# Softmax rows: from sixteen-row tiles in six buffers to thirty-two-row tiles in three, with one broadcast multiply a block

## The chip, the cores and the metric

The kernel runs on one core of one Trainium2 chip. The time is the device time in microseconds (us); most executions of one kernel agree within 0.3% (of the 38 of the kernel before, 162.08 to 163.24 us, 35 lie that close to their median, 162.5 us), and a change is called faster or slower when it is clear of 2%. The profile is one execution; its span is about 2 us shorter than the timed run (160.4 against 162.4 us here). Engines: DVE is VectorE, ACT is ScalarE; the DMA engines (16 of them) move data between HBM and SBUF; SP is the engine from whose queue the loads are issued.

Two executions were in a slower state, one of a_s2half (165.12 us, the fastest of that kernel 162.58) and one of copy64k (166.07 us, the fastest 163.52); they are left out of what follows.

## The reference

```python
x: (16, 1024, 512) float32
x_scaled = x / 0.5
exp_x = np.exp(x_scaled - np.max(x_scaled, axis=-1, keepdims=True))
return exp_x / np.sum(exp_x, axis=-1, keepdims=True)
```

That is 16384 rows of 512, read once and written once: 33.55 MB each way.

## The kernel before

A tile holds 16 rows on each of 128 partitions: 32 KiB a partition, contiguous in HBM, 4 MB in all. There are eight such chunks and six buffers, so the loads of six chunks are issued at the start, and the loads of the last two wait for the stores of the first two. (In the trace the first six go out in seven loads from 0.73 to 4.16 us; for the other two the load queue waited 75.1 us on stores, and the last went out at 88.3 us.) Work goes by blocks of 8 rows: DVE takes the row maxima of a block in one reduce, ACT makes the exponentials and the row sums row by row, DVE inverts the sums and scales three quarters of the rows, ACT scales the last quarter.

```python
G = 16                                              # rows of a partition in a tile
data = ctx.enter_context(tc.tile_pool(name="data", bufs=6))
BLOCKS = [(0, 8), (8, 8)]
...
def scale_vector(i):
    ...
    nc.vector.reciprocal(recip[:, 0:B], sums[:, 0:B])
    for g in range(B - B // 4):                      # one instruction a row
        nc.vector.tensor_scalar_mul(xb[:, g, :], xb[:, g, :], recip[:, g : g + 1])
...
def store(i):                                        # the whole chunk, issued on ACT
    c, b, B = blocks[i]
    if b + B == G:
        nc.scalar.dma_start(out=outr[c], in_=tiles[c])

for i in range(n + 3):
    if i < n:
        if blocks[i][1] == 0:
            load(blocks[i][0])                       # issued on SP
        shift(i)                                     # DVE: reduce, bias
        exponentials(i)                              # ACT
    if 1 <= i <= n:     scale_vector(i - 1)          # DVE
    if 2 <= i <= n + 1: scale_scalar(i - 2)          # ACT copies
    if 3 <= i:          store(i - 3)                 # one block after its copies
```

## Time and profile before

| | before |
|---|---|
| time, median of the first 3 runs | 162.37 us (162.35 to 162.6) |
| span of the profiled run | 160.4 us |
| bytes moved, rate from 4 to 156 us | 67.1 MB, 432 GB/s |
| DVE busy, ACT busy | 114.0 us, 113.1 us |
| first store issued, last store issued | 43.59 us, 137.05 us |

From the page of the kernel before: its span, the busy time of the engines with their share of the span, then rows of 40 equal slices of the span, in which a digit is the busy share in tenths (9 is 90% or more).

```profile
span 160.4 us, 517 instructions
...
DVE 114.0 (71%) x148; ACT 113.1 (70%) x290; POOL 0.2 (0%) x4
...
DVE  0608999999999999999999949996199946000000
ACT  3072579989999999999999995799709999100000
...
DMA  5999999999999999999999999999999999999993
```

The DMA row is full from the second slice to the last but one. DVE and ACT have finished by slice 35, and have holes before. The windows view of the same kernel says it for four stretches late in the run (columns: the stretch and its length, busy time and number of instructions of DVE, ACT and POOL, TensorE clock, DMA share, GB/s):

```profile
core 0: us, DVE busy (x) ACT busy (x) POOL busy (x), PEclk, DMA share, GB/s
60.00:116.00 56.00, 47.96 (x64) 51.40 (x132) 0.00 (x0) 1.00 1.01 437
116.00:120.00 4.00, 4.00 (x1) 0.00 (x0) 0.00 (x0) 1.00 0.95 410
120.00:126.00 6.00, 5.93 (x10) 5.54 (x15) 0.00 (x0) 1.00 1.01 437
126.00:132.00 6.00, 4.09 (x9) 5.83 (x17) 0.00 (x0) 1.00 1.01 437
```

So the kernel is bound by its transfers: 67.1 MB at 432 GB/s is 155 us, and the start and the end cost about 5 us more. The group of the multiplies by shape (count, then busy us and mean ns of one, then idle time before them), and the waits (us in total, times, longest):

```profile
L91 DVE TENSOR_SCALAR xt<-xt,recip 128x512 f32<-128x512 f32 x96 | 39.6, 482 | 0.6
```

```profile
ACT xt L75 <- DVE bias L67: 23.2, 16, 5.7
DVE negmax L65 <- DMA xt<-in_x_dram: 16.9, 4, 5.0
```

The multiplies show 482 ns each, but they overlap: the chain has six of them in 2.47 us, 0.41 us a row. The reduce of 4096 elements a partition takes 4.34 us in the chain, one element in 1.06 ns. Both from the chain (start, length, what):

```profile
27.17 2.47 DVE xt L91 x6
29.63 4.34 DVE negmax L65
```

ACT waits for DVE's bias 16 times; DVE waits for the loads, and only once, for 3.2 us, for ACT: of the two, DVE sets the pace.

### The profile page before, as it was taken

What the parts mean: (1) busy time and instruction counts of PE and PEld (TensorE: products, weight loads), DVE (VectorE), ACT (ScalarE), POOL (GpSimd) and SP (SyncE); (2) the same over time, 40 slices, a digit from 0 to 9 for tenths busy, and PEclk for the clock granted to TensorE, in tenths of its full rate; (3) what the DMA queues carried; (4) which work ended last, traced back from release to release, by engine and by line L of the source; (5) the groups of instructions that cost most, each with busy time, mean ns of one, the idle gap of its engine ahead of it and who ended that gap; (6) DMA issues with size and microseconds to landing.
All of it is one profiled execution on the core that took longest, in us unless ns stands there. A gap on an engine that the chain in (4) does not pass through costs nothing.

```text
span 160.4 us, 517 instructions
## 1 busy us (share of the span) xinstructions
DVE 114.0 (71%) x148; ACT 113.1 (70%) x290; POOL 0.2 (0%) x4
## 2 busy tenths in 40 slices
DVE  0608999999999999999999949996199946000000
ACT  3072579989999999999999995799709999100000
POOL 0000000000000000000000000000000000000000
DMA  5999999999999999999999999999999999999993
GB/s 190 464 425 490 392 417 490 403 392 507 409 368 417 386 441 474 392 417 474 417 409 476 417 400 490 417 400 458 441 409 441 458 409 433 458 400 425 474 409 155
DMA packets 2451, 67.13 MB, mean 419 GB/s; under 512 B 272, under 2 KB 272, under 8 KB 272
## 3 DMA queue, kind: packets, MB, share of 16 engines
q1 hardware_dynamic: 1296, 33.56, 49.4%
q10 hardware_dynamic: 1152, 33.55, 48.5%
q14 instruction: 3, 0.02, 0.0%
HBM read 33.55 MB, written 33.55 MB: 418 GB/s over the span
## 4 chain that ended last, share of the span: by engine, by line
DMA 43%; DVE 34%; ACT 7%; issue 1%; SPq 0%
DMA xt<-in_x_dram 24%; DVE negmax L65 23%; DMA out_dram<-xt 19%; DVE xt L91 9%; ACT xt L75 5%; ACT xt L98 2%; DVE bias L67 1%; DVE recip L89 0%; SPq L59 0%
## 5 line engine op out<-in xcount | busy, mean ns | idle before, releaser
L75 ACT ACTIVATE xt<-xt,bias 128x512 f32<-128x512 f32 x128 | 90.5, 708 | 23.2 <-DVE bias L67 23.2
L65 DVE TENSOR_REDUCE negmax<-xt 128x8 f32<-128x4096 f32 (+1 forms) x17 | 70.8, 4163 | 16.9 <-DMA xt<-in_x_dram 16.9
L91 DVE TENSOR_SCALAR xt<-xt,recip 128x512 f32<-128x512 f32 x96 | 39.6, 482 | 0.6
L75 ACT ACTIVATION_READ_ACCUMULATOR xt<-xt,bias 128x1 f32 x128 | 23.9, 187 | 0.0
L98 ACT ACTIVATE xt<-xt,recip 128x512 f32<-128x512 f32 x32 | 21.0, 707 | 0.0
L89 DVE RECIPROCAL recip<-sums 128x8 f32<-128x8 f32 (+1 forms) x17 | 3.3, 192 | 3.2 <-ACT xt L75 3.2
L67 DVE TENSOR_SCALAR bias<-negmax 128x8 f32<-128x8 f32 (+1 forms) x17 | 2.9, 171 | 0.6
L50 ACT ACT_TABLE_LOAD x1 | 1.3, 1283 | 0.7 <-PEq L134 0.7
L49 DVE MEMSET warm<- 128x1 f32 x1 | 0.1, 59 | 0.8 <-PEq L134 0.8
L50 ACT ACTIVATE warm<-warm 128x1 f32<-128x1 f32 x1 | 0.2, 203 | 0.0
L134 POOL MEMSET const-bfloat16-1.0<- 128x1 bf16 x1 | 0.1, 102 | 0.0
L134 POOL MEMSET const-uint8-127<- 128x1 uint8 x1 | 0.1, 101 | 0.0
L134 POOL MEMSET const-float32-0.0<- 128x1 f32 x1 | 0.1, 99 | 0.2 <-issue 0.2
L134 POOL MEMSET const-float32-1.0<- 128x1 f32 x1 | 0.1, 98 | 0.0
## 6 DMA issues: line engine op xcount, KB each, us to landing
out_dram<-xt ACTq DMA_DIRECT2D x8, 4096.0 KB, 26.2
xt<-in_x_dram SPq DMA_DIRECT2D x7, 4096.0 KB, 30.3
xt<-in_x_dram SPq DMA_DIRECT2D x1, 3072.0 KB, 11.5
xt<-in_x_dram SPq DMA_DIRECT2D x1, 1024.0 KB, 4.7
```

What stands on the lines that cost most here:

```text
L49: nc.vector.memset(warm, 0.0)
L50: nc.scalar.activation(out=warm, in_=warm, func=EXP)
L65: nc.vector.tensor_reduce(negmax[:, 0:B], xb, axis=AX, op=MAX, negate=True)
L67: nc.vector.tensor_scalar_mul(bias[:, 0:B], negmax[:, 0:B], 2.0)
L75: nc.scalar.activation(out=xb[:, g, :], in_=xb[:, g, :], func=EXP, bias=bias[:, g : g + 1], scale=2.0, accum_out=sums[:, g : g + 1],)
L89: nc.vector.reciprocal(recip[:, 0:B], sums[:, 0:B])
L91: nc.vector.tensor_scalar_mul(xb[:, g, :], xb[:, g, :], recip[:, g : g + 1])
L98: nc.scalar.activation(out=xb[:, g, :], in_=xb[:, g, :], func=COPY, scale=recip[:, g : g + 1])
L134: nc = _bacc.Bacc("TRN2", target_bir_lowering=False, num_devices=1)
```

## The change

The intent: fewer and larger instructions and transfers. Tiles of 32 rows (64 KiB pieces in HBM) in three buffers, the same 24 MB; blocks of 16 rows; one multiply a block, with the reciprocals broadcast along the row; a first load of one row; the fourth chunk loaded by halves into the first one's place as its halves are stored. Chunks 1 and 2 are loaded and stored whole, 8 MB each. The diff, cut to its core:

```diff
-    G = 16
+    G = 32
...
+    LOADS = [[(0, 1), (1, 4), (4, 16), (16, G)], WHOLE, WHOLE, HALVES]
+    BLOCKS = [[(0, 4), (4, 8), (8, 16), (16, G)], HALVES, HALVES,
+              [(0, 16), (16, 24), (24, G)]]
+    STORES = [HALVES, WHOLE, WHOLE, HALVES]
+    BUFS = 3
...
-        for g in range(B - B // 4):
-            nc.vector.tensor_scalar_mul(xb[:, g, :], xb[:, g, :], recip[:, g : g + 1])
+        rows = chunks[c][:, lo : lo + k, :]
+        nc.vector.tensor_mul(
+            rows, rows, recips[i][:, 0:k].unsqueeze(2).broadcast_to((P, k, D))
+        )
...
-    for i in range(n + 3):       # shift, exponentials; scale_vector(i - 1);
-        ...                      # scale_scalar(i - 2); store(i - 3)
+    shift(0)
+    shift(1)
+    exponentials(0)
+    for i in range(n):
+        if i + 1 < n:
+            exponentials(i + 1)
+        scale_vector(i)
+        scale_scalar(i)
+        if i + 2 < n:
+            shift(i + 2)
+        store(i)
```

In ACT's program a block's copies, and then the store that ends with it, stand behind the exponentials of the next block, that is of 16 rows. The blocks are numbered 0 to 10: 0 to 3 are chunk 0, 4 and 5 chunk 1, 6 and 7 chunk 2, 8 to 10 chunk 3.

More of the change, by code (lines that the diff above doesn't have):

```diff
@@ L36 @@
     outr = of.rearrange("(c p g) d -> c p g d", p=P, g=G)
-    FIRST = [(0, 4), (4, 16)]
-    BLOCKS_FIRST = [(0, 4), (4, 4), (8, 8)]
-    BLOCKS = [(0, 8), (8, 8)]
-    data = ctx.enter_context(tc.tile_pool(name="data", bufs=6))
+    WHOLE = [(0, G)]
+    HALVES = [(0, 16), (16, G)]
+    LOADS = [[(0, 1), (1, 4), (4, 16), (16, G)], WHOLE, WHOLE, HALVES]
+    BLOCKS = [
+        [(0, 4), (4, 8), (8, 16), (16, G)],
+        HALVES,
+        HALVES,
+        [(0, 16), (16, 24), (24, G)],
+    ]
+    STORES = [HALVES, WHOLE, WHOLE, HALVES]
+    BMAX = 16
+    BUFS = 3
+    data = ctx.enter_context(tc.tile_pool(name="data", bufs=BUFS))
     stats = ctx.enter_context(tc.tile_pool(name="stats", bufs=6))
@@ L50 @@
     nc.scalar.activation(out=warm, in_=warm, func=EXP)
-    tiles = {}
-    blocks = [(c, b, B) for c in range(C) for b, B in (BLOCKS if c else BLOCKS_FIRST)]
-    state = {}
+    chunks = {}
+    blocks = [(c, lo, hi) for c in range(C) for lo, hi in BLOCKS[c]]
+    n = len(blocks)
+    biases, sums, recips = {}, {}, {}
     def load(c):
-        xt = tiles[c] = data.tile([P, G, D], fp32, name="xt")
-        for lo, hi in FIRST if c == 0 else [(0, G)]:
+        if c < BUFS:
+            chunks[c] = data.tile([P, G, D], fp32, name="xt")
+        else:
+            chunks[c] = chunks[c - BUFS]
+        xt = chunks[c]
+        for lo, hi in LOADS[c]:
@@ L59, in load @@
             nc.sync.dma_start(out=xt[:, lo:hi, :], in_=xr[c][:, lo:hi, :])
     def shift(i):
-        c, b, B = blocks[i]
-        xb = tiles[c][:, b : b + B, :]
-        negmax = stats.tile([P, 8], fp32, name="negmax")
-        nc.vector.tensor_reduce(negmax[:, 0:B], xb, axis=AX, op=MAX, negate=True)
-        bias = stats.tile([P, 8], fp32, name="bias")
-        nc.vector.tensor_scalar_mul(bias[:, 0:B], negmax[:, 0:B], 2.0)
-        state[i] = (xb, bias)
+        c, lo, hi = blocks[i]
+        if c not in chunks:
+            load(c)
@@ L70, in exponentials @@
+        b = hi - lo
+        negmax = stats.tile([P, BMAX], fp32, name="negmax")
+        nc.vector.tensor_reduce(
+            negmax[:, 0:b], chunks[c][:, lo:hi, :], axis=AX, op=MAX, negate=True
+        )
+        biases[i] = stats.tile([P, BMAX], fp32, name="bias")
+        nc.vector.tensor_scalar_mul(biases[i][:, 0:b], negmax[:, 0:b], 2.0)
     def exponentials(i):
-        B = blocks[i][2]
-        xb, bias = state[i]
-        sums = stats.tile([P, 8], fp32, name="sums")
-        for g in range(B):
+        c, lo, hi = blocks[i]
@@ L75, in exponentials @@
+        sums[i] = stats.tile([P, BMAX], fp32, name="sums")
+        for g in range(hi - lo):
+            row = chunks[c][:, lo + g, :]
             nc.scalar.activation(
-                out=xb[:, g, :],
-                in_=xb[:, g, :],
+                out=row,
+                in_=row,
                 func=EXP,
-                bias=bias[:, g : g + 1],
+                bias=biases[i][:, g : g + 1],
                 scale=2.0,
-                accum_out=sums[:, g : g + 1],
+                accum_out=sums[i][:, g : g + 1],
@@ L82, in exponentials @@
             )
-        state[i] = (xb, sums)
     def scale_vector(i):
-        B = blocks[i][2]
-        xb, sums = state[i]
-        recip = stats.tile([P, 8], fp32, name="recip")
-        nc.vector.reciprocal(recip[:, 0:B], sums[:, 0:B])
-        for g in range(B - B // 4):
-            nc.vector.tensor_scalar_mul(xb[:, g, :], xb[:, g, :], recip[:, g : g + 1])
-        state[i] = (xb, recip)
+        c, lo, hi = blocks[i]
+        b = hi - lo
+        k = b - b // 4
+        recips[i] = stats.tile([P, BMAX], fp32, name="recip")
@@ L94, in scale_scalar @@
+        nc.vector.reciprocal(recips[i][:, 0:b], sums[i][:, 0:b])
+        rows = chunks[c][:, lo : lo + k, :]
+        nc.vector.tensor_mul(
+            rows, rows, recips[i][:, 0:k].unsqueeze(2).broadcast_to((P, k, D))
+        )
     def scale_scalar(i):
-        B = blocks[i][2]
-        xb, recip = state[i]
-        for g in range(B - B // 4, B):
+        c, lo, hi = blocks[i]
+        b = hi - lo
+        for g in range(b - b // 4, b):
+            row = chunks[c][:, lo + g, :]
             nc.scalar.activation(
-                out=xb[:, g, :], in_=xb[:, g, :], func=COPY, scale=recip[:, g : g + 1]
+                out=row, in_=row, func=COPY, scale=recips[i][:, g : g + 1]
@@ L100, in scale_scalar @@
             )
     def store(i):
-        c, b, B = blocks[i]
-        if b + B == G:
-            nc.scalar.dma_start(out=outr[c], in_=tiles[c])
-    n = len(blocks)
-    for i in range(n + 3):
-        if i < n:
-            if blocks[i][1] == 0:
-                load(blocks[i][0])
-            shift(i)
-            exponentials(i)
-        if 1 <= i <= n:
-            scale_vector(i - 1)
-        if 2 <= i <= n + 1:
-            scale_scalar(i - 2)
-        if 3 <= i:
-            store(i - 3)
+        c, _, end = blocks[i]
@@ L123 @@
+        for lo, hi in STORES[c]:
+            if hi == end:
+                nc.scalar.dma_start(
+                    out=outr[c][:, lo:hi, :], in_=chunks[c][:, lo:hi, :]
+                )
+    shift(0)
[9 more added lines that the diff above has]
+        store(i)
 _INS = ['x']
```

## The prediction

> **What bounds the kernel now.** The DMA engines. The page's slice row shows DMA at 9 tenths in all but the first and last slice; the windows view gives 432 GB/s from 4 to 156 us, and 436, 427, 430 and 433 in the read-only, mixed, late and write-only stretches. 67.1 MB at 432 GB/s is 155.4 us; start and end add about 5: the span of 160.4. DVE (114.0 us busy) and ACT (113.1) have slack; the waits view shows DVE as the tighter: ACT waited 23.2 us for the bias. The timed run is about 2 us longer than the span.
>
> **What the change moves.**
> - Multiply: before, six TENSOR_SCALAR of 128x512 took 2.47 us, 0.41 us a row. After, one tensor_tensor a block. [...] this trace shows 1x in the reduce, 4096 elements in 4.34 us. Estimate: 6144 elements 6.4 to 6.5 us in place of 4.9; the group grows from 39.6 to about 52 us, DVE busy to 125 to 127 us.
> - Reduces of 16 rows: about 8.6 us each; no saving.
> - ACT: the same 160 row instructions, about 113 us.
> - DMA: same bytes, rows of 64 KiB in place of 32; I expect 425 to 436 GB/s again. The first 256 KB piece saves nothing: the second reduce still waits for the 3 MB piece, near 12.7 us.
> - Granularity is what counts. The same 24 MB are resident, but chunks 1 and 2 are stored whole (8 MB), and a store follows its own copies, behind the exponentials of the next block.
>
> **The critical path, estimated from these durations.** I stepped the two in-order engines and two queues through the program. First store at about 45 us, as before (43.6). Third tile landed at 72 to 76 us. From there DVE alternates reduce 8.6, bias 0.2, reciprocal and multiply 6.6: about 15.4 us a block. The store of chunk 1 goes out at 95 to 99 us. All loads and that store are done at 120 to 122 us. The store of chunk 2 needs the next block's exponentials (11.3 us, after that block's reduce, ready near 113 to 115 us) and four copies, 2.5 us: it goes out at 127 to 129 us. So the DMA engines, always fed before, stand empty 6 to 11 us. After that 16.8 MB (39 us) remain without a gap, and nothing wins the time back. Span 169 to 172 us. The slow multiply makes about 3 us of the gap; the rest is store granularity and order.
>
> **Predicted time:** 172.5 us, 80% range 167.5 to 176.5. Faster by over 2%: 0.02; within 2%: 0.07; slower by over 2%: 0.91.
>
> **What would show each step.**
> - Multiplies: 6.4 to 6.6 us for 128x6144. At 4.9 us or less, the 1x step is wrong.
> - Slice row: DMA full until about 120 us, then one or two slices of 0 to 6 tenths, full again from about 130.
> - Chain of waits: back from the last stores through copies, exponentials, reduces and multiplies to the third tile's load.
> - DMA rate in 12 to 43 us near 436 GB/s; otherwise the 64 KiB rows matter.
> - DMA issues: 8 MB stores near 97 and 128 us, landing after 22 to 27 us.
>
> **What would make it wrong.** Queues sharing unevenly, so the third tile lands far from 74 us; ACT's store issue running ahead; [...] 64 KiB rows changing the DMA rate by several per cent. With the gap closed the time would be about 162 us, as the bytes are the same; so I see no way to over 2% faster.

In the prediction, "1x" is the pace of the reduce in the trace before, 4096 elements in 4.34 us. That the broadcast multiply would go at this pace was the author's estimate; no trace had shown it yet.

## The result, and the profile after

| | before | after |
|---|---|---|
| time, median | 162.49 us (162.35 to 163.01, 4 runs) | 170.24 us (169.98 to 171.0, 4 runs) |
| span | 160.4 us | 168.2 us |
| DVE busy, ACT busy | 114.0, 113.1 us | 125.7, 112.5 us |
| DMA share from 120 to 126 us, by the windows view | 1.01 | 0.00 |

The ratio is 1.0479 (95% interval 1.0438 to 1.052): slower by 4.8%. Ratios in this document are the mean time of one kernel's fast runs over the mean of the other's of the same rounds, so not quite the ratio of the medians quoted. The page of the changed kernel:

```profile
span 168.2 us, 414 instructions
...
DVE 125.7 (75%) x45; ACT 112.5 (67%) x290; POOL 0.2 (0%) x4
...
DVE  0509999940999999999999999999999994500000
ACT  3153486399608995999599879959998999300000
...
DMA  5999999699978898989898998999306999598985
```

The DMA row has a hole in slices 29 to 31, with no byte counted in slice 30; elsewhere it is nearly full. (Its scattered 8s, 6s and 5s do not add up to a lower rate: over long stretches it is that of before, as the next fence shows.) The windows, the same stretches as before:

```profile
core 0: us, DVE busy (x) ACT busy (x) POOL busy (x), PEclk, DMA share, GB/s
60.00:116.00 56.00, 55.73 (x16) 49.14 (x128) 0.00 (x0) 1.00 1.02 434
116.00:120.00 4.00, 4.00 (x2) 4.00 (x13) 0.00 (x0) 1.00 0.79 344
120.00:126.00 6.00, 5.76 (x4) 6.00 (x17) 0.00 (x0) 1.00 0.00 0
126.00:132.00 6.00, 6.00 (x2) 5.53 (x15) 0.00 (x0) 1.00 0.81 350
```

The rate from 60 to 116 us is 434 GB/s, against 437 before. From 116 to 132 us these shares leave the DMA engines idle for 0.21 x 4 + 6 + 0.19 x 6 = 8.0 us. That is a rough figure, because the view seems to count a packet where it begins: from 120 to 126 us it shows a share of 0.00, though the store of chunk 1 landed only at 122.7 us (26.7 us after its issue, by the profile's view of that line), and from 132 to 138 us it shows 1.21. A sum over the whole run is safer: by the view of the DMA queues the packets took 97.9% of 160.4 us before, 157.0 us, and 93.9% of 168.2 us after, 157.9 us. So of the 7.8 us by which the span grew, 6.9 are idle time of the DMA engines and 0.9 are packets that took longer. Nearly all of the loss is this hole. The groups and the waits:

```profile
L108 DVE TENSOR_TENSOR xt<-xt,recip 128x6144 f32<-128x6144 f32 x6 | 39.3, 6558 | 0.2
```

```profile
ACT xt L91 <- DVE bias L84: 30.2, 9, 6.1
DVE negmax L80 <- DMA xt<-in_x_dram: 15.6, 3, 6.4
```

A multiply of 6144 elements takes 6.56 us in place of 12 x 0.41 = 4.9. Who made the hole is seen in the timeline (start, length, what; rows left out; ACTq is the part of ACT that issues):

```profile
95.96 0.34 ACTq L125 DMA_DIRECT2D out_dram<-xt  x1
...
104.27 8.68 DVE L80 TENSOR_REDUCE negmax<-xt 128x16 f32<-128x8192 f32 x1
...
113.19 0.72 ACT L91 ACTIVATE xt<-xt,bias 128x512 f32<-128x512 f32 x1 [1.72 <-DVE bias L84]
...
124.49 2.54 ACT L117 ACTIVATE xt<-xt,recip 128x512 f32<-128x512 f32 x4
...
127.06 0.34 ACTq L125 DMA_DIRECT2D out_dram<-xt  x1
```

The store of chunk 1 went out at 95.96 us and the next one, of chunk 2, at 127.06. The second needs the copies of block 7, which start at 124.49, because ACT first makes the 16 exponentials of block 8, which could start only at 113.19, after DVE's reduce of block 8 (104.27) and its bias. By then the queues are empty. And from the chain that ended last, in order of time (it is followed back from DVE's last instruction, and so leaves out the last stores):

```profile
2.57 39.47 DMA xt<-in_x_dram
...
42.06 8.70 DVE negmax L80
...
51.14 6.56 DVE xt L108
57.70 8.61 DVE negmax L80
...
104.35 8.61 DVE negmax L80
...
113.19 8.61 ACT xt L91 x25
```

Rows in between, more of the same, are cut. There is no wait in it from 42.06 us, when chunk 1 had landed whole, to 113 us: DVE works without a break, 15.55 us a block (8.6 reduce, 0.35 bias and reciprocal, 6.56 multiply).

### The profile page after: what moved, and what is told of

It is laid out like the page before. It is cut to its first block, busy times and chain, and to the rows that moved or that the text cites. A ratio compares the mean times of both kernels' runs of the same rounds, so it can differ in the third digit from the quotient of the medians.

```text
span 168.2 us, 414 instructions
## 1 busy us (share of the span) xinstructions
DVE 125.7 (75%) x45; ACT 112.5 (67%) x290; POOL 0.2 (0%) x4
## 4 chain that ended last, share of the span: by engine, by line
DVE 51%; DMA 23%; ACT 10%; SPq 1%; issue 1%
DVE negmax L80 28%; DMA xt<-in_x_dram 23%; DVE xt L108 21%; ACT xt L91 10%; SPq L72 1%; DVE recip L106 1%; DVE bias L84 1%
## 5 line engine op out<-in xcount | busy, mean ns | idle before, releaser
L80 DVE TENSOR_REDUCE negmax<-xt 128x16 f32<-128x8192 f32 (+2 forms) x11 | 69.9, 6353 | 15.6 <-DMA xt<-in_x_dram 15.6
L108 DVE TENSOR_TENSOR xt<-xt,recip 128x6144 f32<-128x6144 f32 (+2 forms) x11 | 52.9, 4812 | 0.4
L117 ACT ACTIVATE xt<-xt,recip 128x512 f32<-128x512 f32 x32 | 20.5, 706 | 0.0
L106 DVE RECIPROCAL recip<-sums 128x16 f32<-128x16 f32 (+2 forms) x11 | 2.4, 219 | 2.6 <-ACT xt L91 2.6
L84 DVE TENSOR_SCALAR bias<-negmax 128x16 f32<-128x16 f32 (+2 forms) x11 | 1.9, 173 | 0.4
```

Of the source, the lines that this page charges most:

```text
L80: nc.vector.tensor_reduce(negmax[:, 0:b], chunks[c][:, lo:hi, :], axis=AX, op=MAX, negate=True)
L84: nc.vector.tensor_scalar_mul(biases[i][:, 0:b], negmax[:, 0:b], 2.0)
L106: nc.vector.reciprocal(recips[i][:, 0:b], sums[i][:, 0:b])
L108: nc.vector.tensor_mul(rows, rows, recips[i][:, 0:k].unsqueeze(2).broadcast_to((P, k, D)))
L117: nc.scalar.activation(out=row, in_=row, func=COPY, scale=recips[i][:, g : g + 1])
```

## The experiments

The theories were these. Theory 1 is the prediction: the hole comes mostly of the size of the stores and their place in the program, and the slow multiply makes about 3 us of it. Theory 2: DVE's pace sets when the store of chunk 2 goes out, so the multiply makes nearly all of it. Theory 3: the 64 KiB pieces, or three buffers, slow the transfers themselves. Each kernel was timed against the kernel before in the same rounds.

| run | what differs from the changed kernel | median us of fast runs | ratio to before (95%) | span us | first store of chunk 2 issued, us |
|---|---|---|---|---|---|
| after | nothing | 170.24 | 1.0479 (1.0438 to 1.052) | 168.2 | 127.06 |
| a_ts | one tensor_scalar a row again | 164.41 | 1.0103 (1.0087 to 1.0119) | 162.5 | 121.34 |
| a_s2half | chunk 2 stored in halves | 162.8 | 1.0011 (0.9983 to 1.004) | 161.0 | 111.61 |
| a_l1half | chunk 1 loaded in halves | 167.89 | 1.0309 (1.0288 to 1.0331) | 166.2 | 125.13 |
| a_l2half | chunk 2 loaded in halves | 170.32 | 1.0488 (1.0473 to 1.0504) | 168.1 | 127.08 |
| a_order | copies before the next exponentials, stores of chunks 2 and 3 on SP | 163.89 | 1.0104 (1.0055 to 1.0154) | 163.5 | 120.41 |
| a_st32k | each 8 MB store cut in two, same place | 165.23 | 1.0164 (1.0144 to 1.0184) | 163.7 | 121.81 |
| a_row32k | pieces of 32 KiB, same transfers | 171.66 | 1.056 (1.0536 to 1.0585) | 169.6 | 128.31 |
| a_halves_ts | per-row multiply, all loads and stores of chunks 1 and 2 in halves | 162.69 | 1.0012 (0.9999 to 1.0026) | 160.9 | 101.42 |
| b_tt | kernel before with the broadcast multiply | 163.12 | 1.002 (1.0005 to 1.0035) | 161.3 | none |

Three more runs, of transfers alone, are below.

### The multiply undone (a_ts)

```diff
-        nc.vector.tensor_mul(rows, rows, recips[i][:, 0:k].unsqueeze(2).broadcast_to(...))
+        for g in range(k):
+            row = chunks[c][:, lo + g, :]
+            nc.vector.tensor_scalar_mul(row, row, recips[i][:, g : g + 1])
```

> The changed kernel with the multiply undone: one tensor_scalar a row, everything else kept. Theory 1 (the prediction): the slow multiply makes about 3 us of the 8 us, so about 167 us. Theory 2 (the pace of VectorE sets when the store of chunk 2 goes out, and each of the four 16-row multiplies between the landing of chunk 1 and that store costs 1.6 us): the store goes out about 6 us earlier, near 121 us, and the time falls to 163 to 165 us. Theory 3 (64 KiB rows or three buffers slow the DMA itself): stays within 1 us of 170.2.

Measured: 164.41 us, 5.8 us less than the change by the medians, 5.7 by the spans. Theory 2's number, not theory 1's 3 us. The timeline of this run has the store of chunk 2 at 121.34 us, which is 5.7 us earlier than 127.06: the span follows the time of issue one for one. The gain is not the full 4 x 1.6 = 6.4 us, because with the fast multiply ACT sets the pace in place of DVE. The chain of this run goes through ACT from 51 us until past that store, and four blocks lie between these two rows:

```profile
51.23 8.61 ACT xt L91 x25
...
107.59 8.50 ACT xt L91 x25
```

That is 14.09 us a block in place of 15.55, and four times the difference is 5.8 us. A loss of 1% remains (ratio 1.0103): the DMA share of this run is 0.76 from 116 to 120 us and 0.81 from 120 to 126.

### The multiply alone, in the kernel before (b_tt)

```diff
-        for g in range(B - B // 4):
-            nc.vector.tensor_scalar_mul(xb[:, g, :], xb[:, g, :], recip[:, g : g + 1])
+        k = B - B // 4
+        rows = xb[:, 0:k, :]
+        nc.vector.tensor_mul(rows, rows, recip[:, 0:k].unsqueeze(2).broadcast_to((P, k, D)))
```

> The kernel before with only the multiply of the change: one broadcast tensor_mul for the six rows of a block, 3.3 us in place of 2.47. Theory 1: the kernel before is bound by DMA with slack behind it, so 162 to 163 us. Theory 2: VectorE's period grows from 7.1 to about 8.0 us a block, the stores go out later, the DMA engines run dry for 0 to 5 us near 130 us; 163 to 167 us. Theory 3: 162.4, since rows and buffers are as before.

Measured: 163.12 us, ratio 1.002. DVE's busy time rose from 114.0 to 128.2 us, more than in the changed kernel, and the time hardly moved: the windows view has the DMA share at 0.98 from 126 to 138 us and 0.86 from 138 to 146, a dent of about 1 us in place of the hole. The ranges do not part the theories here (162 to 163 us and 163 to 167); the size of the effect does. The slow multiply is not enough by itself: it costs 0.2% in this kernel, since with stores of 4 MB the DMA engines still have work when a store comes late. Theory 2 in its plain form ("the multiply is the cause") falls here, as theory 1's 3 us fell above.

### Chunk 2 stored in halves (a_s2half)

```diff
-    STORES = [HALVES, WHOLE, WHOLE, HALVES]
+    STORES = [HALVES, WHOLE, HALVES, HALVES]
```

> The changed kernel with chunk 2 stored in two halves in place of whole (the slow multiply, the whole loads and the 64 KiB rows of chunks 1 kept). Theories 1 and 2: the first half can go out after block 6, near 112 us, before the DMA engines run dry near 119 us, and the second half at 127 us joins a busy queue: no empty stretch, 162 to 163.5 us. Theory 3: about 170.

Measured: 162.8 us, ratio 1.0011, with the slow multiply left in. The first half of chunk 2 went out at 111.61 us, before the queue was empty. Its issue (from the timeline), and the same three late windows in this run:

```profile
111.61 0.34 ACTq L125 DMA_DIRECT2D out_dram<-xt  x1
...
116.00:120.00 4.00, 4.00 (x2) 4.00 (x13) 0.00 (x0) 1.00 0.81 352
120.00:126.00 6.00, 5.76 (x5) 6.00 (x17) 0.00 (x0) 1.00 0.99 426
126.00:132.00 6.00, 6.00 (x2) 5.53 (x15) 0.00 (x0) 1.00 0.96 415
```

The empty stretch is gone, and with it the loss. This is the smallest edit that undoes the result. Together with the two runs above it shows that the loss needs both: a late store, and a store that leaves nothing else queued while it is late.

### Where the chain starts (a_l1half, a_l2half)

```diff
-    LOADS = [[...], WHOLE, WHOLE, HALVES]
+    LOADS = [[...], HALVES, WHOLE, HALVES]     # a_l1half
+    LOADS = [[...], WHOLE, HALVES, HALVES]     # a_l2half
```

> The changed kernel with chunk 1 loaded in two halves, all else kept. If the chain starts at the whole load of chunk 1 (the reduce waited 6.4 us for it until 42.06 us), the reduces start near 36 us, until the load of chunk 2 near 70 us gates the next one: the store of chunk 2 goes out 3 to 4 us earlier, 166 to 167.5 us. If the chain starts at the load of chunk 2, as the prediction had it: 170.2 stays.

> Control to the run with chunk 1 in two loads: here chunk 2 alone is loaded in two halves. Since the reduce of chunk 2 began right after a multiply, without a wait for its load, nothing should move: 169.5 to 170.5 us. If the chain began at the load of chunk 2, as the prediction had it, 166 to 168 us.

Measured: 167.89 us with chunk 1 in two loads (a little above the 166 to 167.5 expected), 170.32 with chunk 2 in two. So the chain began at the whole load of chunk 1, on which DVE stood idle until 42.06 us, and not at the load of chunk 2, where the prediction put it. With chunk 1 in two loads DVE does run into the load of chunk 2; the chain of that run shows it, as a wait of 4.22 us which the profile can't put a name to, right before the reduce of chunk 2's first half:

```profile
60.42 6.56 DVE xt L108
66.98 4.22 another core or an unknown queue
...
71.22 8.70 DVE negmax L80
```

That is why the gain stopped at 2 us of the 6.4 that DVE had waited. (The end of the load is inferred: the reduce needs nothing else that was still open.)

### The order in the program (a_order)

```diff
-                nc.scalar.dma_start(
+                (nc.scalar if c < 2 else nc.sync).dma_start(
...
-        if i + 1 < n:
-            exponentials(i + 1)
         scale_vector(i)
         scale_scalar(i)
+        if i + 1 < n:
+            exponentials(i + 1)
```

> The changed kernel with the order on ScalarE turned round: the copies of a block come before the exponentials of the next block, and the stores of chunks 2 and 3 are issued from the queue of the loads, so that they do not wait in ScalarE's program; slow multiply and whole stores kept. If the empty stretch comes of where the store stands in the program, the store of chunk 2 goes out when its last multiply ends, near 120 us in place of 127, and the time is 163 to 164.5 us. If only VectorE's speed or the size of the stores counts: within 1 us of 170.2.

Measured: 163.89 us (163.2 to 165.25; the profiled execution, span 163.5, was the slowest of the four). The store went out at 120.41 us, when block 7's multiply ended, with the slow multiply and the whole stores kept (from the timeline):

```profile
113.78 6.56 DVE L108 TENSOR_TENSOR xt<-xt,recip 128x6144 f32<-128x6144 f32 x1
...
120.41 0.34 SPq L125 DMA_DIRECT2D out_dram<-xt  x1
```

So the place of the store in the program is worth about 6 us too. The run changes two things at once, the order on ACT and the queue of the late stores; what each is worth alone was not tried. And this is a remedy, not a part of what the change made worse, since the kernel before has its stores at least as far back in ACT's program and shows no hole.

### Cutting the store at the same place (a_st32k), a miss

```diff
-                nc.scalar.dma_start(out=outr[c][:, lo:hi, :], in_=chunks[c][:, lo:hi, :])
+                for a in range(lo, hi, 16):
+                    nc.scalar.dma_start(out=outr[c][:, a : a + 16, :], in_=chunks[c][:, a : a + 16, :])
```

> The changed kernel with each 8 MB store cut into two stores of 16 rows, both issued at the place of the whole one: 32 KiB pieces at unchanged times of issue. If only the time of issue counts: 169.5 to 170.7 us. If the 64 KiB pieces of the stores slow the transfers: 2 us less or more.

Measured: 165.23 us, 5 us less than the change. This would say that long pieces are slow. It doesn't, because the experiment failed to hold what it meant to hold: the time of issue. From ACT's timeline in this run (rows of the sum reads left out):

```profile
121.69 0.71 ACT L91 ACTIVATE xt<-xt,bias 128x512 f32<-128x512 f32 x1
121.81 0.34 ACTq L126 DMA_DIRECT2D out_dram<-xt  x1
...
123.80 0.71 ACT L91 ACTIVATE xt<-xt,bias 128x512 f32<-128x512 f32 x1
...
124.51 2.54 ACT L117 ACTIVATE xt<-xt,recip 128x512 f32<-128x512 f32 x4
127.08 0.34 ACTq L126 DMA_DIRECT2D out_dram<-xt  x1
```

The first half went out at 121.81 us, before three exponentials and four copies that stand ahead of it in ACT's program. It needs only rows that were finished long before, so it did not have to wait until those copies were done, as the whole store must; the issuing part of ACT ran ahead of the computing part, and this store went out 5.27 us before the one behind it (127.08). At that moment one exponential was running and seven instructions were behind it, if the reads of the row sums, which the profile lists as rows of their own, are not counted. The store of chunk 1 shows the same in this run: its first half went out at 90.69 us, with one exponential running and the same seven ahead of it, its second half at 95.97. How far ahead the issue can run was not tried. The store of chunk 2 was 5.25 us early, and the span 4.5 us shorter: once more the time of issue.

### The length of the pieces (a_row32k), and the transfers alone

The clean form of the same question deals the rows of the input to the partitions in another way, so that each row of a tile is two pieces of 32 KiB; sizes, number and places of the transfers stay.

```diff
-    xr = xf.rearrange("(c p g) d -> c p g d", p=P, g=G)
+    xr = xf.rearrange("(c j p g) d -> c p j g d", j=2, p=P, g=16)   # out likewise
```

> The changed kernel with every transfer of 8 MB kept as one, issued at the same places, but the rows of the input dealt to the partitions so that each row of a tile is two pieces of 32 KiB in HBM in place of one of 64 KiB. If the long pieces cost nothing: 169.8 to 170.6 us, the store of chunk 2 near 127 us. If they are a second cost, as the run of transfers alone hints (164.2 against 161.7 us, but there the sizes of the transfers differ too): 168 to 169.5 us.

Measured: 171.66 us, 1.4 us more than the change and above both ranges expected, with the store of chunk 2 1.25 us later: DVE's reduce of chunk 2 began at 74.41 us in the chain in place of 73.25, after a wait of 0.82 us that the profile can't name, presumably for the load. In the changed kernel the long pieces cost nothing that this run shows. The other three are kernels which only load and store, with a wrong result: copy32k has the transfers of the kernel before, copy64k those of the change, copy_row32k those of the change in pieces of 32 KiB.

```diff
-    for i in range(n + 3):
-        ...
+    for c in range(C):
+        load(c)
+        nc.scalar.dma_start(out=outr[c], in_=tiles[c])
```

> The loads and stores of the kernel before alone, no arithmetic, so a wrong result on purpose: each chunk is stored as soon as it has landed. It measures the floor that the transfers set. If the kernel before is bound by the DMA engines and nothing else: 161 to 163 us. If its arithmetic costs time too, clearly less, say 155 us.

> The loads and stores of the changed kernel alone, no arithmetic, wrong on purpose: rows of 64 KiB, three buffers, whole stores. Theory 3 (the long rows or the three buffers slow the transfers): 166 to 170 us. Theories 1 and 2: the same as the run with 32 KiB rows within 1.5 us.

> Transfers of the changed kernel alone (wrong on purpose), sizes, buffers and order kept, pieces of 32 KiB in place of 64. If the 2.4 us between the two runs of transfers alone come of the length of the pieces: 161.5 to 162.3 us. If they come of the larger transfers and fewer buffers: near 164.2 us.

Measured:

| run | median us of fast runs | ratio to before (95%) |
|---|---|---|
| copy32k | 161.74 | 0.9956 (0.9939 to 0.9973) |
| copy64k | 163.62 | 1.0098 (1.0061 to 1.0135) |
| copy_row32k | 162.62 | 1.0002 (0.9977 to 1.0028) |

Two things follow. The transfers of the kernel before take 161.74 us without any arithmetic, so all its reduces, exponentials and multiplies cost it 0.4%: no change of the arithmetic could have gained 2%. And with nothing else in the kernel, pieces of 64 KiB cost about 1% against the same transfers in pieces of 32 KiB. That is theory 3 at about a fifth of the loss; a_row32k doesn't show it in the changed kernel, and a_s2half, which keeps the long loads and the long store of chunk 1, is at 1.0011. How much of it acts there stays open; the two runs of transfers came from different calls, and copy64k has only three fast executions, from 163.52 to 164.71 us. The expectations were missed here: copy64k lies 1.9 us above copy32k, where theories 1 and 2 allowed 1.5 and theory 3 began at 166 us, and copy_row32k lies between the two values given for it.

### What the runs point to (a_halves_ts)

> The changed kernel with the fast multiply, and all loads and stores in halves of 16 rows (32 KiB pieces): what the experiments point to. The DMA engines should never be empty: 161.5 to 163 us, the same as the kernel before (ratio 0.995 to 1.003). Faster by more than 1% would say that the transfers were not the floor.

Per-row multiplies and all loads and stores of chunks 1 and 2 in halves: 162.69 us against 162.51, ratio 1.0012. It equals the kernel before and does not beat it, as a kernel at the floor of its transfers must (161.74 us for the transfers alone, in copy32k). It also keeps three buffers of 64 KiB a partition, so three buffers cost nothing that this run shows.

## Why the prediction was right

The prediction was 172.5 us with a range of 167.5 to 176.5, slower by over 2% at 0.91. Measured: 170.24 us, slower by 4.8%. Point by point:

- **"What bounds the kernel now. The DMA engines."** Right, and shown by copy32k: 161.74 us for the transfers alone.
- **"6144 elements 6.4 to 6.5 us in place of 4.9; the group grows from 39.6 to about 52 us".** 6.56 us by the group's mean, 52.9 us in all, DVE busy 125.7 us (125 to 127 predicted). The estimate took the pace of the reduce: 4.34 us for 4096 elements makes 6.51 for 6144, and the multiply came within 1% of that. The three sizes in the trace, 6558, 3358 and 1758 ns for 6144, 3072 and 1536 elements, differ by 1.04 ns an element and leave about 0.16 us a multiply beside it.
- **"I expect 425 to 436 GB/s again."** 434 from 12 to 43 us and from 60 to 116 us. Alone, the long pieces cost about 1%; the prediction named this only as a risk, of several per cent.
- **"the DMA engines, always fed before, stand empty 6 to 11 us".** 6.9 us more idle time than before, by the sum over the run. Wholly without work they were for less, from 122.7 to 127.06 us; the share falls off before that. The store of chunk 1 went out at 95.96 us (95 to 99 predicted), the store of chunk 2 at 127.06 (127 to 129 predicted); they landed after 26.7 and 20.9 us (22 to 27 predicted).
- **"All loads and that store are done at 120 to 122 us"**: close, since the store of chunk 1 landed at 122.7 us.
- **"Third tile landed at 72 to 76 us. From there DVE alternates ..."** Wrong in where the chain starts. DVE was busy without a break from the landing of chunk 1 at 42.06 us, and never waited for the third tile; a_l1half gained 2.4 us, a_l2half nothing. The tile had in fact landed by 70.9 us: its load was issued before 3.65 us and took 67.2, the longest of all loads in the profile's view of the tile. The time of issue still came out right because DVE reached chunk 2 at 73.2 us by its own pace, about when the prediction let the tile land. That the two agree is luck.
- **"The slow multiply makes about 3 us of the gap; the rest is store granularity and order."** Mis-sized, and wrong as a sum. The multiply is worth 5.7 us here (a_ts), the size of the store about 7 (a_s2half), its order about 6 (a_order). These don't add up to 7.8, because each alone closes most of the hole. The step that failed follows from the last point: the prediction put the start of the chain at the third tile's landing, and after it only two multiplies come before block 8's reduce, 2 x 1.6 = 3.2 us, which fits its "about 3 us". Four lie on the chain from 42.06 us, 4 x 1.6 = 6.4 us, of which ACT's pace lets 5.7 through (a_ts).
- **The point was 2.3 us too high** because each step's middle was taken and the trace lay at the early end of each: 127.06 of 127 to 129 for the issue, then 41.1 us to the end of the span. This last term is nearly the same in other runs with one whole store of chunk 2 and ACT's order as it was: 41.1 us after 125.13 (a_l1half), 41.2 after 121.34 (a_ts), 41.3 after 128.31 (a_row32k). In a_order it is 43.1 after 120.41, in the slowest of its executions.

## What to carry to other kernels

In a kernel at the floor of its transfers an engine's busy time means little (in b_tt DVE's rose by 14.2 us and the time by 0.2%); what counts is whether something is still queued each time that a store is late. Compare the time at which the queued transfers will be finished with the time at which the next store can be issued. Here the larger store moved the second back, from 111.61 us for the first half of chunk 2 (a_s2half) to 127.06 for the whole, and left nothing in between: the queued transfers had landed at 122.7. Ask of each part of a change whether it is enough alone, since parts that share one hole each seem to be worth most of it (5.7, about 7 and about 6 us here, of 7.8), and check in the trace that an experiment held what it meant to hold.
